# Loading and normalizing the second group of rows between the modulation weights

## The chip, the cores and the metric

The kernel runs on one core of one Trainium2 chip. The metric is device time in microseconds (us) of one launch; lower is better. TensorE is written PE, VectorE DVE, ScalarE ACT, GpSimd POOL and SyncE SP, as in the rows below; SP issues every DMA of this kernel, in one order.

## What is computed

One inference step of a one-layer encoder for two request groups: 1024 prompt rows and 64 sample rows of width 1024, all in 32-bit floats. The part around the change is the first RMS norm, its modulation, and the projection:

```
def modulate(c, w_ada, b_ada):
    m = jax.nn.silu(c) @ w_ada + b_ada
    return jnp.split(m[:, None, :], 6, axis=-1)     # shift1, scale1, gate1, shift2, scale2, gate2
def pre(x, g, shift, scale):
    return rmsnorm(x, g) * (1.0 + scale) + shift
u = pre(x, g_pre_mix, shift1, scale1) @ w_in        # q | k | v of 4 differential, 8 stick-breaking heads
...
x = x + gate1 * rmsnorm(mix @ w_out, g_post_mix)
x = x + gate2 * rmsnorm(square(relu(h2 @ w_up)) @ w_down, g_post_ffn)
```

## The kernel before

Rows go through in nine tiles x0 to x8 of 128 (x8 holds the 64 sample rows), in three groups g of three tiles: x0 to x2, x3 to x5, x6 to x8. Every product is made of three matmuls on a high and a low part of each operand (`split`, lines 62 to 65: a cast on ACT gives the high part, a subtraction on DVE or POOL the low part). The hidden rows are kept transposed, in eight blocks k of 128 columns, as `h1h` and `h1l`.

The start of the kernel is a pipeline over the adaLN weights that make shift1 and scale1, 8 MB in sixteen tiles of 512 KB (`ada_raw`, lines 128 to 136). They come in quarters q = 0 to 3 of four tiles; quarter q gives the shift and scale (`A1`, `B1`) of blocks 2q and 2q+1. For each quarter PE multiplies the weights by silu(c) (`ada_rows`, line 201, tile `pam`), DVE copies the sums to `Rm` (line 322), PE turns them into columns (line 209, tile `pcm`), DVE finishes `A1` and `B1` (lines 326 to 328), and DVE and ACT write the modulated blocks `xt` (lines 344, 346) and split them. Then `first(k)` (line 357) multiplies block k of the first group by the q, k and v weights of head unit 0 into three PSUM banks `p00`, `p01`, `p02`, which fill up over all eight blocks (lines 303 to 305).

`norm_inplace` (line 153) is the RMS norm of a tile of rows: two squares with a running sum on ACT (line 87), three small operations on POOL (lines 89, 80, 81), and two scalings by the result on DVE (line 158). For x0 to x2 it stands before the weights. For x3 to x5 it stood at the head of `ready_1` (line 579), which then transposes the second group (line 335), modulates and splits it, with the low parts on POOL. x6 to x8 are normed after that.

The code is not run in the order in which it is written: the framework schedules the whole program with a timing model of its own when it is built and fixes each engine's order from it. Buffers of one tag are taken from a free pool: the tag `qk` has ten, which the first ten weight tiles, the rows x3 to x7, and the Q and K tiles share; the last six weight tiles lie in the tag `h` as `ae0` and `ae1`. SP issues at most eight transfers ahead: each one waits for the landing of the one eight places earlier. After the projections come the attention units 0 to 7, the output projection, and the feed-forward layer.

Of the kernel before, what the change touches and what calls it, by code (L numbers as in the profile page):

```python
# [27 lines left out]
NTT = 9  # L28
# [6 lines left out]
def build(tc, I, O):  # L35
# [11 lines left out]
    def big(name, tag, shape, dt=F32R):  # L47
        return sb.tile(shape, dt, tag=tag, name=name, bufs=BUFS[tag])

    def small(shape, name, tag, dt=F32, bufs=2):  # L50
        return sb.tile(shape, dt, tag=tag, name=name, bufs=bufs)
# [4 lines left out]
    def bank(name, tag):  # L56
        return pp.tile([P, 512], F32, tag=tag, name=name)
# [9 lines left out]
    def halves(name, n=2):  # L67
        return [big(f"{name}_{i}", "s", [P, 512], F32) for i in range(n)]
# [9 lines left out]
    def rstd(ss, rows, name, add=EPS, inv=1.0 / D):  # L78
        r = small([P, 1], name, "rs", bufs=4)
        nc.gpsimd.tensor_scalar(r[:rows], ss, inv, add, ALU.mult, ALU.add)  # L80
        nc.gpsimd.tensor_tensor(r[:rows], r[:rows], mhalf[:rows], ALU.pow)
        return r

    def sumsq(srcs, rows, name, scratch):
        ss = small([P, 2], name, "ss", bufs=4)
        for i, (a, jk) in enumerate(zip(srcs, scratch)):
            nc.scalar.activation(jk[:rows, : a.shape[-1]], a, AF.Square, accum_out=ss[:rows, i : i + 1])
        if len(srcs) == 2:
            nc.gpsimd.tensor_tensor(ss[:rows, 0:1], ss[:rows, 0:1], ss[:rows, 1:2], ALU.add)
        return ss[:rows, 0:1]  # L90
# [5 lines left out]
    def x_rows(m):  # L96
        return (x_p[m * P : (m + 1) * P, :], P) if m < 8 else (x_s, TS)
# [16 lines left out]
    def load_x(m):  # L114
        src, rows = x_rows(m)
        x = big(f"x{m}", "qk" if m < 8 else "v", [P, 1024], F32)
        load(x[:rows], src)
        return [x[:, :512], x[:, 512:]]
# [9 lines left out]
    def ada_raw(q, part, half):  # L128
        n = 4 * q + 2 * part + half
        if n < 10:  # L130
            raw = big(f"ar{q}{part}{half}", "qk", [P, 4, 256], F32)
        else:
            raw = eh[(n - 10) // 3][:, (n - 10) % 3]
        c0 = D * part + 256 * q
        load(raw, w_ada[:, 4 * half : 4 * half + 4, c0 : c0 + 256])
        ada_raws[c0, half] = raw
# [9 lines left out]
    xn = []  # L146
# [6 lines left out]
    def norm_inplace(xs, m):  # L153
        rows = x_rows(m)[1]
        jk = [small([P, 512], f"jk{m}{i}", "ah") for i in range(2)]
        r = rstd(sumsq([x[:rows] for x in xs], rows, f"ssa{m}", jk), rows, f"rsa{m}")
        for x in xs:
            nc.vector.tensor_scalar(x[:rows], x[:rows], r[:rows], None, ALU.mult)
# [29 lines left out]
    def ada_rows(c0, name, ps=None, between=()):  # L188


        if ps is None:
            ps = bank("pa" + name, "pj")[:, :256]
        for q in range(2):
            raw = ada_raws.get((c0, q))
            if raw is None:
                raw = big(f"ar{name}{q}", "raw", [P, 4, 256], F32)
                load(raw, w_ada[:, 4 * q : 4 * q + 4, c0 : c0 + 256])
            if q == 1 and between:
                between.pop()()
            for i in range(4):  # L200
                mm(ps[32 * i : 32 * i + 32], lhsT=sc[:, 4 * q + i, :], rhs=raw[:, i, :], start=(q == 0), stop=(q == 1), skip_group_check=True)
            yield 0.5
        return ps
# [81 lines left out]
    def drain(gen):  # L285
        for _ in gen:
            pass
# [10 lines left out]
    def dense_T(ps, w, act, g, ks=range(KT)):  # L298

        n = GRP[g][1]  # L300
        (wh, wl), (hh, hl) = w, act[g]
        for k in ks:
            mm(ps[:, :n], lhsT=wh[:, k, :], rhs=hh[:, k, :n], start=(k == 0), stop=False)  # L303
            mm(ps[:, :n], lhsT=wh[:, k, :], rhs=hl[:, k, :n], start=False, stop=False)  # L304
            mm(ps[:, :n], lhsT=wl[:, k, :], rhs=hh[:, k, :n], start=False, stop=(k == 7))  # L305
            yield 3 * n / 2400
# [12 lines left out]
    def columns(ps, q):  # L319

        R = big(f"Rm{q}", "s", [P, 512], F32)
        nc.vector.tensor_copy(R, ps)
        v = sum_to_columns(R, 4, f"pcm{q}")
        col = lambda c: colE[:, c + 2 * q : c + 2 * q + 2].unsqueeze(2).broadcast_to([P, 2, 2])
        a, b = A1[:, 2 * q : 2 * q + 2, :], B1[:, 2 * q : 2 * q + 2, :]
        nc.vector.tensor_tensor(a, v[:, 2:4], col(16), ALU.add)
        nc.vector.tensor_tensor(b, v[:, 0:2], col(8), ALU.add)
        nc.vector.scalar_tensor_tensor(a, a, 1.0, col(0), ALU.add, ALU.mult)

    def block_T(g, k, tag):  # L330

        ps = bank(f"px{g}{k}", tag)
        for m in range(3 * g, 3 * g + 3):
            rows, off = x_rows(m)[1], (m % 3) * P
            nc.tensor.transpose(ps[:, off : off + rows], xn[m][k // 4][:rows, (k % 4) * P : (k % 4 + 1) * P], ident[:rows, :rows])
        return ps

    def block_mod(ps, g, k, el=None, on_act=False):
        n = GRP[g][1]
        xt = small([P, 512], f"xt{g}{k}", "al")  # L340
        for j, c in ((0, slice(0, min(n, TP - GRP[g][0]))), (1, slice(256, 320)))[: 1 + (g == 2)]:
            a, b = A1[:, k, j : j + 1], B1[:, k, j : j + 1]
            if on_act and j == 0:
                nc.scalar.activation(xt[:, c], ps[:, c], AF.Identity, bias=b, scale=a)
            else:
                nc.vector.tensor_scalar(xt[:, c], ps[:, c], a, b, ALU.mult, ALU.add)
        hi, lo = (t[:, k, :n] for t in hT[g])
        split(xt[:, :n], hi, lo, el=el)
        if g == 2:
            nc.vector.tensor_tensor(hT[g][0][:, k, 320:384], xt[:, 256:320], fr(hi[:, 256:320]), ALU.subtract)  # L350
# [6 lines left out]
    def first(k):  # L357

        for i in range(3):
            drain(dense_T(PS[i], PW[0, i], hT, 0, (k,)))  # L360
# [6 lines left out]
    def first_weights(half, up=False):  # L367
        ks = slice(4 * half, 4 * half + 4)
        for i in range(3):
            c = unit_cols(0)[i]  # L370
            if up:
                load(w0[i][:, ks], w_in[:, ks, c : c + P])
                continue
            split(w0[i][:, ks], *(t[:, ks] for t in PW[0, i]), el=nc.vector)

    for q in range(4):
        for part, half in ((0, 0), (0, 1), (1, 0), (1, 1)):
            if q + part:
                ada_raw(q, part, half)
        if q < 2:  # L380
            first_weights(q, True)
    pend = []
    for q in range(4):
        if q < 2:
            first_weights(q)
        for k in (2 * q, 2 * q + 1):
            px[k] = block_T(0, k, ("tr", "qk", "pv")[k % 3])
        ps = bank(f"pam{q}", "pj")
        for part in range(2):
            drain(ada_rows(D * part + 256 * q, f"m{q}{part}", ps[:, 256 * part : 256 * part + 256], pend))  # L390

        def work(ps=ps, q=q):
            columns(ps, q)
            for k in (2 * q, 2 * q + 1):
                block_mod(px[k], 0, k, None, k % 2 == 1)

        pend.append(work)
        if q == 3:
            pend.pop()()
        elif q >= 1:  # L400
            first(2 * q - 2)
            first(2 * q - 1)
    for k in range(4, KT):
        first(k)
    xn += [load_x(m) for m in range(3, NTT)]


    lam4 = small([P, 4, 64], "lam4", "ah")
# [168 lines left out]
                PW[u + 1, i] = proj_weights(u + 1, i)  # L577

    def ready_1():
        for m in range(3, 6):  # L580
            norm_inplace(xn[m], m)
        for k in range(KT):
            block_mod(block_T(1, k, "tr"), 1, k, nc.gpsimd, k % 2 == 1)

# [421 lines left out]
    cost = [st.cost for st in steps]  # L1006
    drain(proj(0, 0))
    ready_1()
    for m in range(6, 9):
        norm_inplace(xn[m], m)  # L1010
# [64 lines left out]
    for m in range(NTT):  # L1075
# [25 lines left out]
        xn = halves(f"xn{m}")  # L1101
# [196 lines left out]
```

## Time and profile before

| | |
|---|---|
| median of 3 runs | 1563.65 us (1562.17 to 1564.41) |
| the profiled execution's own time | 1566.6 us |
| its span | 1564.9 us |
| PE busy | 1504.1 us, 96% of the span |
| DVE, ACT, POOL busy | 59%, 45%, 22% |
| DMA moved | 133.20 MB, mean 85 GB/s |

The span runs from the first to the last instruction; 1.7 us of the execution's own time lie around it. In the first 40th of the span PE is 60% busy, and from the third on 90% or more almost throughout. DMA is 90% busy in the first 40th, 30% or less in most others.

### The profile page before, as it was taken

To read this page: it belongs to the slowest core of one execution; us is meant where nothing else is said; L and a number is where in the kernel's file an instruction comes from. 1 tells how busy PE (TensorE), PEld (TensorE's weight loads), DVE (VectorE), ACT (ScalarE), POOL (GpSimd) and SP (SyncE) were. 2 spreads that over 40 slices of the span, in tenths; PEclk is the share of its full clock that TensorE was granted. 3 is DMA by queue.
4 is the path that set the end of the run, shared out by engine and by line. 5 is a ranking of instruction groups with operands and counts; after the bars stand their busy time and mean duration, and the time that the engine had idled before them with its cause. 6 is when DMAs were issued, how large, how long until landed. Compare 5 with 4: busy or idle time off the path is not lost.

```text
span 1564.9 us, 23485 instructions
## 1 busy us (share of the span) xinstructions
PE 1504.1 (96%) x8714; PEld 1344.9 (86%) x8714; DVE 919.8 (59%) x1761; ACT 702.6 (45%) x1650; POOL 339.0 (22%) x519
## 2 busy tenths in 40 slices
PE   6899999999999999799999999999999999999998
PEld 3689898989989888678899988899899899899896
DVE  3776768676768577775553454444554544544447
ACT  3866766667666576656654112212122111221132
POOL 1553443535152323442110000000000000000002
PEclk9999999999999999799999999999999999999999
DMA  9322343433232215343221222111111111111025
GB/s 314 117 61 83 93 120 91 131 94 108 67 97 74 82 59 167 106 139 132 76 60 41 68 81 81 56 53 41 54 54 41 29 42 52 55 53 43 28 81 181
DMA packets 152516, 133.20 MB, mean 85 GB/s; under 512 B 11233, under 2 KB 136274, under 8 KB 152402
## 3 DMA queue, kind: packets, MB, share of 16 engines
q1 hardware_dynamic: 152402, 131.71, 27.4%
q8 instruction: 68, 1.11, 0.3%
q14 instruction: 46, 0.38, 0.1%
HBM read 108.59 MB, written 23.09 MB: 84 GB/s over the span
## 4 chain that ended last, share of the span: by engine, by line
PE 77%; DVE 6%; issue 5%; ACT 4%; POOL 2%; DMA 2%; POOLq 0%; DVEq 0%; ACTq 0%; SPq 0%
PE pu L303 8%; PE pu L305 8%; PE pu L304 8%; PE pd L1173 8%; PE pd L1174 8%; PE pd L1176 7%; PE pt L604 2%; PE pq L303 2%; PE pq L305 2%; PE pq L304 2%; PE pk L304 2%; PE pk L303 2%; PE pk L305 2%; PE pv L303 2%; PE pv L304 2%
## 5 line engine op out<-in xcount | busy, mean ns | idle before, releaser
L1180 DVE TENSOR_TENSOR acc<-pd,acc 128x512 f32<-128x512 f32 x252 | 171.8, 687 | 113.7 <-PE pd L1176 107.9
L1158 ACT ACTIVATE sq<-pu 128x384 f32<-128x384 f32 (+1 forms) x96 | 45.1, 470 | 309.3 <-PE pu L305 309.3
L1159 DVE TENSOR_TENSOR sq<-sq 128x384 f32<-128x384 f32 (+1 forms) x96 | 72.1, 751 | 172.9 <-ACT sq L1158 172.9
L65 DVE TENSOR_TENSOR al<-pt,ah 128x512 fp32r<-128x512 f32 (+2 forms) x128 | 75.3, 599 | 30.7 <-ACT ah L64 28.7
L593 PE MATMUL pz<-K,Q 128*128 128x512 f32 (+2 forms) x192 | 72.2, 378 | 7.4 <-DVE mn L678 2.4
L64 ACT CAST ah<-pt 128x512 fp32r<-128x512 f32 (+2 forms) x128 | 65.4, 521 | 29.5 <-PE pt L604 24.1
L604 PE MATMUL pt<-ident,s 128*128 128x128 f32 x432 | 69.6, 277 | 0.8 <-issue 0.4
L594 PE MATMUL pz<-Kl,qz 128*128 128x512 f32 (+2 forms) x192 | 65.9, 349 | 0.0
L642 ACT ACTIVATE s<-s,mn 128x512 f32<-128x512 f32 (+3 forms) x96 | 58.5, 612 | 15.5 <-DVE mn L678 14.5
L743 DVE TENSOR_TENSOR_SCAN s<-k,s 128x128 f32<-128x128 f32 (+1 forms) x64 | 53.0, 836 | 13.6 <-ACT k L767 7.7
L65 DVE TENSOR_TENSOR rl<-sq,rh 128x384 fp32r<-128x384 f32 x64 | 35.7, 558 | 38.1 <-ACT rh L64 38.1
L766 ACT ACTIVATE s<-pz 128x512 f32<-128x512 f32 (+2 forms) x96 | 47.6, 496 | 20.9 <-PE pz L594 15.5
L604 PEld LDWEIGHTS pt<-ident,s 128*128 128x128 f32 x432 | 50.0, 142 | 3.8 <-issue 0.6
L442 POOL CAST qz<-Q 64x256 fp32r<-64x256 f32 x64 | 31.2, 488 | 92.9 <-PE pz L594 84.0
L593 PEld LDWEIGHTS pz<-K,Q 128*128 128x128 f32 x192 | 36.4, 190 | 17.2 <-DVE mn L678 6.1
L64 ACT CAST rh<-sq 128x384 fp32r<-128x384 f32 x64 | 32.8, 513 | 40.2 <-DVE sq L1159 38.2
L767 ACT ACTIVATE k<-pz 128x512 f32<-128x512 f32 (+2 forms) x96 | 47.7, 497 | 2.0 <-DVE s L743 0.9
L789 PE MATMUL po<-al,V 128*128 128x256 f32 (+1 forms) x160 | 42.3, 299 | 5.3 <-DVE al L65 5.0
L770 POOL TENSOR_SCALAR_AFFINE_SELECT s<-s 128x128 f32<-128x128 f32 x64 | 30.2, 475 | 75.8 <-ACT s L766 75.2
L788 PE MATMUL po<-ah,V 128*128 128x256 f32 (+1 forms) x160 | 44.8, 294 | 0.4 <-DVE ok L467 0.3
L743 DVE TENSOR_TENSOR_SCAN s<-k,s,s 128x512 f32<-128x512 f32 x32 | 43.4, 1355 | 0.4
L64 ACT CAST r<-sq 128x320 fp32r<-128x320 f32 x32 | 14.8, 461 | 62.6 <-DVE sq L1159 62.6
(1232 smaller groups left out, 5145.5 us busy)
## 6 DMA issues: line engine op xcount, KB each, us to landing
arr<-in_w_ada SPq DMA_DIRECT2D x16, 512.0 KB
arm<-in_w_ada SPq DMA_DIRECT2D x16, 512.0 KB
ar<-in_w_ada SPq DMA_DIRECT2D x10, 512.0 KB
mixD<-mx SPq DMA_DIRECT2D x32, 128.0 KB
xr<-in_x_prompt SPq DMA_DIRECT2D x16, 256.0 KB
xD<-xr SPq DMA_DIRECT2D x16, 256.0 KB
xy<-xD SPq DMA_DIRECT2D x8, 512.0 KB
out_y_prompt<-xy SPq DMA_DIRECT2D x16, 256.0 KB
```

The lines of the kernel that those rows point to most:

```text
L64: (eh or nc.scalar.copy)(hi, src)
L65: (el or nc.vector).tensor_tensor(lo, src, fr(hi), ALU.subtract)
L303: mm(ps[:, :n], lhsT=wh[:, k, :], rhs=hh[:, k, :n], start=(k == 0), stop=False)
L304: mm(ps[:, :n], lhsT=wh[:, k, :], rhs=hl[:, k, :n], start=False, stop=False)
L305: mm(ps[:, :n], lhsT=wl[:, k, :], rhs=hh[:, k, :n], start=False, stop=(k == 7))
L593: mm(ps[:, :w], lhsT=S["Q"][m][:, qt], rhs=S["Kd"][m][:, c0 : c0 + w], start=True, stop=False)
L604: nc.tensor.transpose(pt[:kr, i * P : (i + 1) * P], a, ident)
L743: nc.vector.tensor_tensor_scan(d, k, d, 0.0 if c == n - 1 else s[c + 1][:, 0:1], ALU.mult, ALU.add)
L1173: mm(ps, lhsT=rh[:, off : off + P], rhs=wh[:, cols], start=(j == 0), stop=False)
L1174: mm(ps, lhsT=rh[:, off : off + P], rhs=wl[:, cols], start=False, stop=(m == 8 and end))
L1176: mm(ps, lhsT=rl[:, off : off + P], rhs=wh[:, cols], start=False, stop=end)
L1180: nc.vector.tensor_tensor(acc[m][:, cols], ps, acc[m][:, cols], ALU.add)
```

## The change

The loads of x3, x4 and x5 move ahead of the third quarter's weights, and their norm moves from `ready_1` to after the point where the weights of the third quarter (q = 2) are multiplied. Nothing is computed in another way.

```diff
@@ the loop over quarters @@
     for q in range(4):
+        if q == 2:
+            xn += [load_x(m) for m in range(3, 6)]
         for part, half in ((0, 0), (0, 1), (1, 0), (1, 1)):
             if q + part:
                 ada_raw(q, part, half)
...
         elif q >= 1:
             first(2 * q - 2)
             first(2 * q - 1)
+        if q == 2:
+            for m in range(3, 6):
+                norm_inplace(xn[m], m)
     for k in range(4, KT):
         first(k)
-    xn += [load_x(m) for m in range(3, NTT)]
+    xn += [load_x(m) for m in range(6, NTT)]
...
     def ready_1():
-        for m in range(3, 6):
-            norm_inplace(xn[m], m)
         for k in range(KT):
             block_mod(block_T(1, k, "tr"), 1, k, nc.gpsimd, k % 2 == 1)
```

What this does to the schedule shows in three queues. On SP, from the last weights of unit 0 on, before (`ar200`, `ar201`, `ae0`, `ae1` are the eight weight tiles of quarters 2 and 3, `lam4` small constants):

```order
L135 DMA ar200_191<-in_w_ada 128x4x256
L135 DMA ar201_193<-in_w_ada 128x4x256
L135 DMA ae0_78<-in_w_ada 128x4x256 x3
L135 DMA ae1_79<-in_w_ada 128x4x256 x3
L117 DMA x3_457<-in_x_prompt 128x1024
L117 DMA x4_459<-in_x_prompt 128x1024
L117 DMA x5_461<-in_x_prompt 128x1024
L117 DMA x6_463<-in_x_prompt 128x1024
L117 DMA x7_465<-in_x_prompt 128x1024
L117 DMA x8_467<-in_x_sample 64x1024
L410 DMA lam4_469<-in_lambda_q1 128x64
```

and in the changed kernel (`T0` is a table of attention unit 0, `wq1r` and `wk1r` weights of unit 1):

```order
L117 DMA x3_191<-in_x_prompt 128x1024
L117 DMA x4_193<-in_x_prompt 128x1024
L117 DMA x5_195<-in_x_prompt 128x1024
L135 DMA ar200_197<-in_w_ada 128x4x256
L135 DMA ar201_199<-in_w_ada 128x4x256
L135 DMA ae0_78<-in_w_ada 128x4x256 x3
L135 DMA ae1_79<-in_w_ada 128x4x256 x3
L117 DMA x6_496<-in_x_prompt 128x1024
L117 DMA x7_498<-in_x_prompt 128x1024
L117 DMA x8_500<-in_x_sample 64x1024
L884 DMA Tst0_1752<-in_dist_s 128x64
L670 DMA T0_670<-in_dist 128x1024
```

The eight weight tiles stand three places later, x6 to x8 where they stood, and `lam4` behind `T0`, `wq1r` and `wk1r`.

On ACT, in quarters 2 and 3, before (`jk` are the squares of a row tile, `xt` and `h1h` modulation and split, `Q00` and `kf00` the first evictions of the products):

```order
L344 ACTIVATE xt05_387<-px05_303,B1_122,A1_121 128x384
L64 CAST h1h0_115<-xt05_387 128x384
L64 CAST h1h0_115<-xt04_383 128x384
L87 ACTIVATE jk30_538,ssa3_540<-x3_457 128x512
L87 ACTIVATE jk31_539,ssa3_540<-x3_457 128x512
L87 ACTIVATE jk40_549,ssa4_551<-x4_459 128x512
L344 ACTIVATE xt07_417<-px07_364,B1_122,A1_121 128x384
L87 ACTIVATE jk41_550,ssa4_551<-x4_459 128x512
L64 CAST h1h0_115<-xt06_413 128x384
L64 CAST h1h0_115<-xt07_417 128x384
```

and in the changed kernel:

```order
L87 ACTIVATE jk60_635,ssa6_637<-x6_496 128x512
L87 ACTIVATE jk61_636,ssa6_637<-x6_496 128x512
L87 ACTIVATE jk70_646,ssa7_648<-x7_498 128x512
L344 ACTIVATE xt05_426<-px05_309,B1_122,A1_121 128x384
L87 ACTIVATE jk71_647,ssa7_648<-x7_498 128x512
L64 CAST h1h0_115<-xt04_422 128x384
L64 CAST h1h0_115<-xt05_426 128x384
L87 ACTIVATE jk80_657,ssa8_659<-x8_500 64x512
L87 ACTIVATE jk81_658,ssa8_659<-x8_500 64x512
L344 ACTIVATE xt07_456<-px07_403,B1_122,A1_121 128x384
L64 CAST h1h0_115<-xt07_456 128x384
L64 CAST h1h0_115<-xt06_452 128x384
```

The squares of x6 and the first of x7 stand ahead of quarter 2's modulation, those of x8 ahead of quarter 3's; those of x3 to x5 stand earlier still. Before, the last four squares stood behind `Q00`, between the evictions.

On DVE, at the modulation of quarter 1 and at that of quarter 3, the changed kernel has:

```order
L158 TENSOR_SCALAR x3_191<-x3_191,rsa3_372 128x512 x2
L158 TENSOR_SCALAR x4_193<-x4_193,rsa4_383 128x512 x2
L158 TENSOR_SCALAR x5_195<-x5_195,rsa5_394 128x512 x2
L326 TENSOR_TENSOR A1_121<-pcm1_320,colE_112 128x4
L327 TENSOR_TENSOR B1_122<-pcm1_320,colE_112 128x4
L328 SCALAR_TENSOR_TENSOR A1_121<-A1_121,colE_112 128x4
L346 TENSOR_SCALAR xt02_328<-px02_244,A1_121,B1_122 128x384
```

```order
L346 TENSOR_SCALAR xt06_452<-px06_399,A1_121,B1_122 128x384
L158 TENSOR_SCALAR x8_500<-x8_500,rsa8_663 64x512 x2
L419 TENSOR_TENSOR lam4_502<-lam4_502 128x64
L65 TENSOR_TENSOR h1l0_116<-xt07_456,h1h0_115 128x384
L419 TENSOR_TENSOR lam4_502<-lam4_502 128x64
L65 TENSOR_TENSOR h1l0_116<-xt06_452,h1h0_115 128x384
L346 TENSOR_SCALAR xt10_575<-px10_571,A1_121,B1_122 128x384
```

Before, no scaling stood ahead of quarter 1's `A1`, and the first multiply of `lam4` came after both `h1l0` of quarter 3. Further down the order of all engines is changed in small pieces up to attention unit 6, and is the same from there on; the set of instructions is the same.

## Rows read from the trace of the kernel before

**Rows 1.** The page: busy time of PE, and the chain's shares by engine.

```profile
PE 1504.1 (96%) x8714; PEld 1344.9 (86%) x8714; DVE 919.8 (59%) x1761; ACT 702.6 (45%) x1650; POOL 339.0 (22%) x519
...
PE 77%; DVE 6%; issue 5%; ACT 4%; POOL 2%; DMA 2%; POOLq 0%; DVEq 0%; ACTq 0%; SPq 0%
```

**Rows 2.** Busy time by stretch: from:to and its length, five engines, clock, DMA, GB/s.

```profile
14.00:20.00 6.00, 2.54 (x24) 1.01 (x22) 2.58 (x6) 1.85 (x3) 0.00 (x0) 1.00 1.09 359
20.00:25.00 5.00, 4.25 (x34) 2.16 (x35) 2.71 (x8) 1.59 (x3) 0.00 (x0) 0.70 1.11 347
25.00:30.00 5.00, 5.00 (x26) 3.76 (x25) 2.49 (x4) 1.85 (x3) 0.00 (x0) 0.62 1.08 364
...
40.00:50.00 10.00, 9.71 (x76) 8.36 (x76) 6.43 (x18) 8.28 (x21) 3.02 (x9) 1.00 0.89 282
...
55.00:60.00 5.00, 3.74 (x14) 2.84 (x13) 3.40 (x8) 4.93 (x12) 1.99 (x5) 0.66 0.13 39
60.00:70.00 10.00, 9.36 (x56) 8.48 (x57) 8.16 (x22) 7.02 (x19) 7.40 (x8) 1.00 0.01 2
...
510.00:560.00 50.00, 44.00 (x279) 40.34 (x279) 30.58 (x50) 29.26 (x71) 19.18 (x28) 0.91 0.31 93
```

**Rows 3.** Timeline of SP's DMA issues: start, duration, what.

```profile
39.57 0.33 SPq L410 DMA_DIRECT2D lam<-in_lambda_k  x1
40.85 0.33 SPq L410 DMA_DIRECT2D lam<-in_lambda_q  x1
...
43.41 0.33 SPq L881 DMA_DIRECT2D Tst<-in_dist_s  x1
```

**Rows 4.** What SP's issues waited for: us in total, times, longest.

```profile
SPq L410 <- DMA ae<-in_w_ada: 2.0, 2, 1.1
SPq L410 <- DMA x<-in_x_prompt: 1.9, 2, 0.9
```

**Rows 5.** Timeline of PE: quarter 2's first weights, and the first group's products.

```profile
30.78 0.64 PE L201 MATMUL pam<-ar,sc 128*32 128x256 f32 x8
31.35 1.05 PE L209 MATMUL pcm<-sel,Rm 128*128 128x2 f32 x8
...
35.02 0.44 PE L303 MATMUL p<-h1h,w00h 128*128 128x384 f32 x1
...
39.67 1.05 PE L209 MATMUL pcm<-sel,Rm 128*128 128x2 f32 x8
...
42.92 0.44 PE L303 MATMUL p<-h1h,w00h 128*128 128x384 f32 x1 [0.29 <-ACT h1h L64]
...
50.37 0.34 PE L305 MATMUL p<-h1h,w20l 128*128 128x384 f32 x1
```

**Rows 6.** Timeline: norm of x3 from square to scaling; last two scalings.

```profile
42.77 0.62 ACT L87 ACTIVATE jk<-x 128x512 f32<-128x512 f32 x1
...
44.32 0.19 POOL L89 TENSOR_TENSOR ssa<-ssa 128x1 f32<-128x1 f32 x1 [30.60 <-ACT jk L87]
...
45.78 0.87 DVE L158 TENSOR_SCALAR x<-x,rsa 128x512 f32<-128x512 f32 x2
...
54.86 1.63 DVE L158 TENSOR_SCALAR x<-x,rsa 128x512 f32<-128x512 f32 x2
...
60.10 2.26 DVE L158 TENSOR_SCALAR x<-x,rsa 64x512 f32<-64x512 f32 x2
```

**Rows 7.** Groups on ACT, 42 to 60 us: busy us, mean ns, idle before.

```profile
L87 ACT ACTIVATE jk<-x 128x512 f32<-128x512 f32 (+1 forms) x12 | 7.5, 627 | 0.3
...
L87 ACT ACTIVATION_READ_ACCUMULATOR jk<-x 128x1 f32 (+1 forms) x12 | 2.3, 188 | 0.0
```

**Rows 8.** Timeline of ACT: the first eviction, and the second group's last cast.

```profile
50.19 0.47 ACT L488 ACTIVATE Q<-p 64x384 fp32r<-64x384 f32 x1
...
68.53 0.53 ACT L64 CAST h1h<-xt 128x384 fp32r<-128x384 f32 x1
```

## The prediction

> **What bounds the kernel now.** I read the page first: PE is busy 96% of the span and holds 77% of the chain that ended last [rows 1]. Only a change in PE's idle time, or in the clock that it is granted, can move the end. So the next view is busy time by stretch [rows 2]. The start is the loosest part: PE is busy 2.54 of 6 us at 14 to 20 us, while DMA moves 359 GB/s, and 3.74 of 5 us at 55 to 60 us. Between them, from 40 to 50 us, it is nearly full (9.71 of 10), and from 60 to 70 us again (9.36).
>
> Who holds PE in the loose parts? At first the adaLN weights. SP's small loads are a clock for landings, as each waits for the transfer eight places ahead: the issues of `lam4` ended waits on the last weight tiles and on x3 and x4 [rows 4]. They read: last weight tile down at 39.57, x3 at 40.85, x5 at 43.41 [rows 3]. So a row tile takes 1.28 us (40.85 - 39.57), and the longest of the two waits on weights, 1.1 us behind an issue of 0.33, gives about 1.43 for a weight tile of the same size. PE is then late by itself: it starts the last quarter's columns well after the landing and runs products from 42.92 to 50.71 (50.37 + 0.34) almost without a gap [rows 5]. From 50 us the binding engine is ACT: 4.93 us of 5 at 55 to 60 us [rows 2], with the norm's squares among the evictions that PE waits for.
>
> **The change, part by part.** It adds and removes no instruction; all is in the order.
>
> *Loads.* The eight weight tiles of quarters 2 and 3 slide behind three row tiles, 3 x 1.28 = 3.85 us. The last one lands at 43.4 (x5's old place), x6 and x7 land one and two row tiles later, 44.7 and 46.0. The first of the eight comes down four places ahead of the old last weight, with three of the tiles before it being rows: 39.57 - 4 x 1.43 - 3 x 0.15 = 33.4. PE was ready for it at 30.78 [rows 5], so PE stands still for 2.6 us. Behind it in PE's queue stands `pcm` of quarter 1, which has nothing to do with that weight; it slides along, to end at 31.35 + 1.05 + 2.6 = 35.0.
>
> *Scalings of x3 to x5 on DVE.* They stand ahead of quarter 1's `A1`. x3 lands at about 29.4. A tile's two squares take 1.5 us (42.77 to the sum at 44.25; POOL starts at 44.32), and the scaling starts 1.5 us after them, at 45.78, for 0.87 us [rows 6]. Three tiles in a row: squares until 33.9, scaling of x5 at 35.4 to 36.3. So `A1` waits from 35.0 to 36.3, 1.3 us more, and behind it ACT's `xt`, both casts, and PE's products of block 2: 35.02 + 2.6 + 1.3 = 38.9.
>
> *Products of blocks 2 and 3.* From 35.02 to the next `pcm` at 39.67 are 4.65 us, of which one batch of weights, 0.64 [rows 5], now comes earlier: 4.0 us, at full clock. But PE idled before them. [...] Now it idles 2.6 us and, after `pcm`, about 2.4 us more. The price lies between nothing and twelve of eighteen products at half speed, some 1.7 us. I take 1.5, as the stretch of 14 to 20 us is the nearest row. `pcm` of quarter 2 then starts at 38.9 + 4.0 + 1.5 = 44.4, ends at 45.4.
>
> [...]
>
> *Squares of x6 to x8 on ACT.* Quarter 2's `xt` stands behind both squares of x6 and one of x7, so behind x7's landing at 46.0: it starts at 47.0 though `A1` is there at about 46. Another square, 0.82 us (0.627 + 0.188) [rows 7], stands ahead of the casts. The product of block 4 starts at 48.9 instead of 42.92: 6.0 us late. Quarter 3's `xt` stands behind the squares of x8, which have landed by then. DVE's multiply of `lam4` now stands ahead of the last two `h1l0`, and its loads behind three tiles of 512 KB; I put the landing at 52 to 53 and DVE's need at 53, so no cost, but up to 3 us if it comes later. The products end at 50.71 + 6.1 = 56.8.
>
> *What is given back.* After the first eviction `Q00` ACT no longer holds the four squares of x7 and x8: 4 x 0.82 = 3.3 us off the stretch from 50.19 to the last cast of the second group, at 68.53 + 0.53 = 69.06 [rows 8]. In 60 to 70 us ACT was also idle for 10 - 7.02 = 3.0 us [rows 2], waiting for DVE and POOL, whose queues are shorter by the norms too. Going through the new order with these durations I find about 1.8 of the 3.0 used. Given back: 5.1 us.
>
> The sum: 6.1 - 5.1 = +1.0 us on 1566.6 of the profiled execution, 1567.6. That execution lies 2.95 us above the median of 1563.65, so the median comes to 1564.7.
>
> *Bounds.* Above: nothing is given back, +6.1. Below: no half clock (-1.5) and all of ACT's idle time used (3.0 instead of 1.8, -1.2), and 55 to 60 us at full clock instead of 0.66, 5 x 0.34 = 1.7: 1.0 - 4.4 = -3.4, or 1560.3.
>
> On the scalings: the last two pairs took 1.63 and 2.26 us instead of 0.87 [rows 6], while POOL ran the second group's low parts. [...] I keep ACT as the path.
>
> *The order further down.* Up to unit 6 all engines' orders differ in small pieces. No row prices that. PE's idle time by 50 us shows what order does: 6.0 us in the worst of these stretches, with clock 0.91 [rows 2], near zero in others. I take 0 for the mean and 3 us to either side, half the worst one.
>
> **The rivals.** *Slower, no giving back.* Once the products end at 56.8, PE itself is the bound: at 60 to 70 us it was busy 9.36 of 10 [rows 2], so work that comes 6 us later ends 6 us later, whatever ACT has shed. That gives 1569.8. Its place is PE between the last `p` product and the last second-group product; it decides against "same" once less than 3.0 of the 6.1 us come back. For it speaks 9.36; against it the 1.3 us idle at 55 to 60 us and the half clock there.
>
> *Faster, the norms were the path.* The delay is taken up by PE's own lateness (weights landed at 39.57, products ran until 50.71), while ACT and DVE are free of norms when the second group starts: the lower bound, 1560.3. For it speaks ACT at 4.93 of 5; against it that PE was full from 40 to 50 us with products that the weights gate.
>
> *Order alone decides.* The start comes out even and the changed order down to unit 6 gains or loses 3 us: 1561 or 1567.
>
> *It doesn't do what it says.* If x3 to x5 waited for buffers, nothing would come earlier. Their buffers come free with the first weights, multiplied at 11 us, so I give this nothing.
>
> **How the numbers follow.** About 0.2%, 3.1 us, is what a measurement of this kernel can tell from no change: 1560.5 to 1566.8. The forecast, within that, has 0.54. Slower has 0.29: 0.16 for the rival that gives nothing back, 0.13 for order. Faster has 0.17: 0.08 for the norms, 0.09 for order. The range from 1560.0 to 1569.8 reaches from just under the lower bound to the slower rival; past it lies some 0.1 at either end, where order adds to a rival.
>
> **What the profile after would show.** The loads: the first weight product of quarter 2 at about 33.4 instead of 30.78. DVE: scalings until about 36 and `A1` right behind. ACT: squares of x6 and x7 ahead of `xt` at 47. The products ending at about 56.8; the second group's last cast at about 70. If that cast is at 75, nothing came back; if at 66, the norms were the path. A difference that arises only after 110 us is order. I am wrong in mechanism if the products end before 54, which would mean that weights did not gate PE.

## The result, and the profile after

The changed kernel takes 1585.78 us (median of 4 runs, 1585.24 to 1586.88), the kernel before 1564.03 beside it: a ratio of 1.0137, interval 1.0123 to 1.0151, or 21 us slower. I had forecast 1564.7 and a range that ended at 1569.8. The profiled execution took 1586.88 us, with a span of 1585.1, 20.2 more than before.

The page of the changed kernel, first PE's busy time and the chain's shares [rows 1]:

```profile
PE 1513.1 (95%) x8714; PEld 1353.3 (85%) x8714; DVE 926.9 (58%) x1761; ACT 702.0 (44%) x1650; POOL 338.3 (21%) x519
...
PE 75%; DVE 7%; issue 6%; ACT 5%; POOL 2%; DMA 1%; POOLq 0%; DVEq 0%; ACTq 0%
```

PE holds the chain as before. It is busy 9.0 us more (1513.1 - 1504.1), with the same 8714 matmuls, so it ran slower (a mean granted clock of 0.978 over the span, 0.985 before); and it is idle 11.2 us more, the rest of the 20.2.

Where this arises shows best in the time at which PE starts its n-th matmul, counted in either trace (not always the same matmul, as the orders differ, but as much work). In us, the time in the kernel before, and how much later it is in others (three of them are experiments, told below):

| n | 400 | 600 | 1000 | 1400 | 1800 | 2200 | 2600 | 3000 | 3400 |
|---|---|---|---|---|---|---|---|---|---|
| before | 84 | 117 | 178 | 236 | 297 | 360 | 419 | 482 | 544 |
| changed kernel | +0.9 | +7.1 | +10.2 | +13.1 | +15.9 | +17.0 | +19.8 | +21.8 | +21.0 |
| changed start, order of before | +3.0 | +3.4 | +3.4 | +3.4 | +3.4 | +5.3 | +5.3 | +5.4 | +6.0 |
| start of before, changed order | -3.4 | +2.5 | +5.7 | +8.5 | +11.5 | +11.0 | +14.1 | +14.7 | +15.6 |
| order of before from unit 3 on | +1.6 | +7.8 | +10.9 | +13.7 | +18.4 | +18.4 | +18.4 | +18.3 | +17.7 |

At 84 us, where the start is over, the changed kernel is 0.9 us late. The lag grows in nearly every stretch from there to 480 us and stays where it is afterwards; PE's order differs from that of before up to 523 us. Each row is one execution, and whole executions of one kernel lay 1.6 us (the changed kernel) to 8.2 us (the changed start with the order of before) apart, so a step of 1 or 2 us says little. The row of the start of before with the changed order begins at -3.4: by this count the changed order is the better one up to 84 us, and from there to 544 us it loses 19.0 us (15.6 + 3.4).

### The profile page after: what moved, and what is told of

Read it like the earlier page. It is cut to its first block, busy times and chain, and to the rows that moved or that the text cites. A ratio compares the mean times of both kernels' runs of the same rounds, so it can differ in the third digit from the quotient of the medians.

```text
span 1585.1 us, 23509 instructions
## 1 busy us (share of the span) xinstructions
PE 1513.1 (95%) x8714; PEld 1353.3 (85%) x8714; DVE 926.9 (58%) x1761; ACT 702.0 (44%) x1650; POOL 338.3 (21%) x519
## 4 chain that ended last, share of the span: by engine, by line
PE 75%; DVE 7%; issue 6%; ACT 5%; POOL 2%; DMA 1%; POOLq 0%; DVEq 0%; ACTq 0%
PE pu L303 8%; PE pu L305 8%; PE pu L304 8%; PE pd L1176 8%; PE pd L1177 8%; PE pd L1179 7%; PE pt L607 2%; PE pq L303 2%; PE pq L304 2%; PE pq L305 2%; PE pk L305 2%; PE pk L303 2%; PE pk L304 2%; DVE s L746 2%; PE pv L303 1%
## 5 line engine op out<-in xcount | busy, mean ns | idle before, releaser
L681 DVE CUSTOM_DVE_ANT_0 s<-pz,T 128x512 f32<-128x512 f32 (+3 forms) x64 | 37.1, 586 | 11.6 <-PE pz L597 11.0
```

## Order or start: the two taken apart

**How an order is held.** The framework lets an edge be put between two instructions of one engine that fixes which is issued first and adds no wait. A table gives the order of one kernel for everything written from the projections of unit 0 on, norms excepted, and each instruction gets an edge to the one ahead of it on its engine. The start stays as the framework lays it out. Holding costs little by itself: the kernel before, held in its own order but for one small group of instructions, takes 1564.91 us (ratio 1.0008), and the changed kernel, held in its own order but for one place, 1586.13; both are told below.

```diff
-        build(tc, I, O)
+        build(tc, I, O); hold_order(tc)
...
+def hold_order(tc):
+    insts = tc.nc.cur_bb.bb.instructions
+    a, b, c, d, e = marks
+    part = insts[a:b] + insts[c:d] + insts[e:]
+    dep = mybir.DependencyInfo(mybir.DependencyClass.NoSync, mybir.DependencyReason.DATA)
+    for t in HELD.values():
...
+        for x, y in zip(at, at[1:]):
+            tc.add_manual_dep(part[y], part[x].name, dep, reason="order")
```

**The changed start with the order of before.** (`HELD` is before's order.)

> The changed kernel, loads and norms as in the change, but every instruction written from the projections of unit 0 on (other than the norms) is held, engine by engine, in the order of the kernel before. Theory 'order': the start leaves the second group's last cast 2.8 us later (71.85 instead of 69.06), and the other 17 to 18 us come from the changed order of units 0 to 6; so this kernel takes about 1567 us (1564 to 1570). Rival 'start': the late start itself, with its buffers and transfers shifted, makes everything behind it stall, whatever the order; so this stays near 1585 us. In between, say 1575, both have a share.

Measured: 1571.48 us, ratio 1.0038 (1.0023 to 1.0052), 5.9 us by the ratio.

**The start of before with the changed order.** (The kernel before; `HELD` is the changed kernel's order.)

> The other way round: the start of the kernel before, with everything from the projections of unit 0 on held in the order of the changed kernel. Theory 'order': the order brings its loss along, 1564 + 17 to 18 = about 1582 us (1578 to 1586). Rival 'start': near 1564 us.

Measured: 1578.19 us, ratio 1.0099 (1.0075 to 1.0123), 15.5 us. The two parts, 0.38% and 0.99%, make the 1.37% of both together: start and order add, and the order is nearly three quarters of the loss. Theory "order" held, with its share some 2 us smaller and the start's some 3 us larger than it said (1571.48 lies just above its range, 1578.19 at the lower end of its range).

Busy time by stretch, 85 to 510 us, where the orders differ throughout (engines PE, PEld, DVE, ACT, POOL, then granted clock, DMA share, GB/s). The kernel before, then the changed start with the order of before:

```profile
85.00:510.00 425.00, 415.61 (x2793) 380.65 (x2792) 306.60 (x771) 292.71 (x800) 172.03 (x273) 1.00 0.32 94
```

```profile
85.00:510.00 425.00, 415.58 (x2770) 380.36 (x2769) 303.39 (x764) 291.89 (x798) 169.27 (x271) 0.99 0.31 92
```

The same for the changed kernel, then for the start of before with the changed order:

```profile
85.00:510.00 425.00, 403.94 (x2641) 368.98 (x2641) 296.14 (x738) 274.21 (x759) 163.18 (x261) 0.97 0.30 90
```

```profile
85.00:510.00 425.00, 404.00 (x2658) 369.84 (x2659) 298.84 (x736) 279.45 (x770) 160.91 (x259) 0.98 0.30 90
```

The first number after the length is PE's busy time, the one in brackets its matmuls. With the old order PE is busy 415.6 us in both kernels, with the new one 404.0 in both, whatever the start. In the changed kernel 152 matmuls fewer (2793 - 2641) are done in these 425 us, at 0.149 us each (415.61 / 2793) work for 22.6 us. Of these 11.7 are idle time (425 - 403.94, less 425 - 415.61); the other 10.9 were lost with PE busy, at a clock of 0.97 instead of 1.00. So about half of the loss is waits and half is slow matmuls.

What PE waited for in that stretch, the longest rows (us in total, times, longest), in the changed kernel:

```profile
PE pz L596 <- DVE mn L681: 5.0, 8, 2.4
PE pt L607 <- DVE s L746: 2.5, 1, 2.5
PE ptS L607 <- DVE ss L734: 2.3, 1, 2.3
```

and with the start of before:

```profile
PE pz L593 <- DVE mn L678: 5.3, 7, 2.8
PE pt L604 <- DVE s L743: 2.5, 1, 2.5
PE ptS L604 <- DVE ss L731: 2.5, 1, 2.5
```

The same waits, line by line (numbers of lines shift by 3). In the kernel before, the first of these stands at 1.1 us, and the other two are not among its longest:

```profile
PE pz L593 <- DVE mn L678: 1.1, 4, 0.4
```

**The old order from unit 3 on.** Here only the instructions written from the loop step of unit 3 on are held, by the same means.

> The changed kernel, in which only the instructions written from the loop step of unit 3 on are held in the old order; what lies ahead is free, as in the change. Where unit 3 begins (about 253 us before) the changed kernel is 12.8 us late, at 480 us 22. If the loss is a sum of losses in each stretch, each with its own place in the order, this gives about 1564 + 13 = 1577 us (1574 to 1580). If a lag, once there, feeds further lag in any order, it comes to 1583 or more; if the old order makes up for lag, below 1572.

Measured: 1579.92 us, ratio 1.0106 (1.0079 to 1.0133). The last row of the lag table is this run: the lag grows like the changed kernel's until the instructions of unit 3 take over, 18.4 us at n = 1800, and from there not at all. PE does not get later by being late; each stretch of the order has its own losses. (The profiled execution lies 2.5 us above the changed kernel at n = 1800; this kernel's four executions lie up to 4.9 us apart.)

## Is it this order, or any new one?

Three more orders, laid out freely by the framework. In the first only the loads are moved:

```diff
@@ the changed kernel, loop over quarters @@
-        if q == 2:
-            for m in range(3, 6):
-                norm_inplace(xn[m], m)
@@ ready_1 @@
     def ready_1():
+        for m in range(3, 6):
+            norm_inplace(xn[m], m)
```

> Of the change only the early loads of x3 to x5; their norm stays at the head of ready_1, and the order is free, so it is a third order for units 0 to 6. By 'order' the time can fall anywhere that an order can put it: the start costs some 3 us (the weights land 3.4 us later), and the order adds 0 to 20, so 1567 to 1587, with no reason to equal the changed kernel's. By 'start' it follows the weights: 1567.

Measured: 1577.71 us, ratio 1.0094 (1.0074 to 1.0114). The framework set the squares of x3 to x5 ahead of quarter 1's modulation all the same, because the rows are there: the second half of the change, writing the norm earlier, moves next to nothing at the start. It does make another order further down.

In the second and third, the eviction of K takes its two halves the other way round, first in the kernel before, then in the changed one:

```diff
@@ proj_k @@
-        for m in range(2):
+        for m in (1, 0):
             r, o = slice(64 * m, 64 * m + 64), slice(64 - 64 * m, 128 - 64 * m)
             nc.scalar.copy(Kd[m][r, cols], ps[r, :w])
```

> The kernel before, with its start untouched, and one edit that means nothing for the work: of the two halves of K the one with index 1 is evicted first. The framework lays out another order for units 0 to 6 (the first PE instruction that differs is behind the start). Theory 'any new order costs': the order of before is far better than a usual one, and this loses 10 to 18 us as the other two new orders did, 1574 to 1582. Rival 'the new order of the change was bad luck': orders lie around that of before, 1564 with some 5 us to either side.

Measured: 1572.31 us, ratio 1.0052 (1.0030 to 1.0073): 8 us for an edit without meaning for the result and with the start untouched (PE's order is that of before up to 54 us). What the swap costs in an order that is otherwise that of before was not run.

> The changed kernel with the meaningless edit of the other order experiment: of the two halves of K the one with index 1 is evicted first, the order is free. If the 14 to 18 us of the changed order are one draw of many, another order gives another loss: start 6 plus 4 to 18, so 1574 to 1588, most likely not within 3 us of 1585.8. If the change's late start makes any freely laid out order bad, it stays at 1583 to 1589.

Measured: 1578.38 us, ratio 1.0096 (1.0078 to 1.0115), 6 us faster than the changed kernel by the ratios. If the start costs 5.9 in these too, which was not measured, the four free orders lost about 15 (the change), 9 (the loads alone), 8 and 9 us against the order of before. None was as good. How many would be is not known from four. Shown is that a small edit, even one without meaning, can give the order of before away, and that this costs more than any start tried here.

## One place in the new order

The largest step of the lag, 6.2 us between n = 400 and n = 600, is one place. Timeline of the changed kernel at 100 us, PE, DVE and POOL (start, duration, what, idle before and releaser):

```profile
101.86 0.63 PE L597 MATMUL pz<-Kl,qz 128*128 128x512 f32 x1
104.87 0.76 PE L596 MATMUL pz<-K,Q 128*128 128x512 f32 x1 [2.38 <-DVE mn L681]
...
107.18 0.47 PE L305 MATMUL pv<-h1h,w20l 128*128 128x320 f32 x1
```

```profile
101.40 1.68 DVE L647 TENSOR_TENSOR l<-l 128x1 f32<-128x1 f32 x1
...
104.02 0.69 DVE L681 CUSTOM_DVE_ANT_0 s<-pz,T 128x512 f32<-128x512 f32 x1
```

```profile
100.70 2.36 POOL L65 TENSOR_TENSOR wk1l<-wk1r,wk1h 128x1024 fp32r<-128x1024 f32 x1
```

and the busy times of 102 to 110 us, with PE's granted clock, in the same columns as above:

```profile
102.00:110.00 8.00, 5.62 (x21) 4.77 (x20) 6.41 (x16) 4.00 (x12) 2.86 (x5) 0.50 0.36 121
```

DVE's order has the sum `l` ahead of the next score's reduction. `l`, one column, took 1.68 us and ended with POOL's split of a weight (100.70 + 2.36 = 103.06); behind it stood its reciprocal, `cf`, an eviction of Q, and then at 104.02 the reduction for which PE's next score waited, 2.38 us. PE's granted clock was 0.50 from 102 to 110 us, and 16 of the 24 `pv` products took 0.47 or more instead of 0.31. It did not fall behind this wait: it stood at 0.50 from 100.8 us on, after PE had been idle for 0.16, 0.24 and 0.52 us between the scores ahead.

```profile
100.80:102.50 1.70, 1.69 (x3) 0.68 (x3) 1.56 (x3) 1.65 (x7) 1.70 (x1) 0.50 0.56 164
```

With the start of before and the changed order both rows are there again, on DVE and on PE:

```profile
97.09 1.68 DVE L644 TENSOR_TENSOR l<-l 128x1 f32<-128x1 f32 x1 [0.17 <-ACT s L642]
```

```profile
100.56 0.77 PE L593 MATMUL pz<-K,Q 128*128 128x512 f32 x1 [2.85 <-DVE mn L678]
```

In the kernel before, DVE has the reduction ahead of `l`, and PE has the transposes `pnk` and four pairs of `po` between the scores (DVE's rows, then PE's):

```profile
101.80 0.69 DVE L678 CUSTOM_DVE_ANT_0 s<-pz,T 128x512 f32<-128x512 f32 x1
...
102.42 0.15 DVE L644 TENSOR_TENSOR l<-l 128x1 f32<-128x1 f32 x1
```

```profile
99.50 0.44 PE L459 MATMUL pnk<-ident,kf 128*128 128x128 f32 x2
...
102.65 0.47 PE L593 MATMUL pz<-K,Q 128*128 128x512 f32 x1 [0.74 <-DVE l L644]
103.08 0.41 PE L303 MATMUL pv<-h1h,w20h 128*128 128x320 f32 x1
```

So I changed this one place: the changed kernel's own order held, but with two moves in the tables. On PE the 24 `pv` products go ahead of the waiting score `pz`; on DVE the eviction of Q and the reduction go ahead of the sum `l`.

> The changed kernel, its own order held from the projections of unit 0 on, but for one place at 100 us. There DVE had the sum l, its reciprocal and cf ahead of an eviction of Q and a score's reduction, PE waited 2.38 us for that reduction, its clock fell from 101 to 111 us, and the 24 matmuls of pv, which stood behind the wait, ran at half speed. Here DVE does Q and the reduction first, and PE has the 24 pv matmuls ahead of the waiting score. Theory 'stalls and their clock': the lag that arises between 84 and 117 us falls from 6.2 us to about 0, and the end comes 5 to 6 us earlier, about 1580 us. Rival 'the time is only moved': another wait takes its place within some 20 us, and the end stays within 1.5 us of 1585.8.

Measured: 1586.13 us, ratio 1.0133 (1.0113 to 1.0153). The rival held. The trace of this kernel shows the wait that took its place, on PE and then on DVE:

```profile
104.40 0.63 PE L303 MATMUL pv<-h1h,w20h 128*128 128x320 f32 x1 [3.04 <-DVE Kl L519]
```

```profile
102.02 0.15 DVE L647 TENSOR_TENSOR l<-l 128x1 f32<-128x1 f32 x1
...
103.92 0.43 DVE L519 TENSOR_TENSOR Kl<-pk,K 64x256 fp32r<-64x256 f32 x1
```

`l` now takes 0.15 us and the reduction is done at 102.02, but `pv` waits 3.04 us for a PSUM bank that the second eviction of K (`Kl`, 103.92) holds, and runs at a clock of 0.50 (102 to 109 us) as before, 0.47 us for a product. PE has nothing else there: the `po` pairs that filled this stretch in the kernel before stand ahead of it in the new order, `pnk` behind it. So one instruction in front of another was not the cause. That the cause is which work is left for PE when ACT and DVE are behind fits these rows, but it is argued: no run put the `po` pairs or `pnk` back there.

## The start by itself

With the order of before held, the start costs 5.9 us, not the +1.0 of my sum. Two edits to it. In the first the squares of x6 to x8 are kept behind quarter 3's casts on ACT:

```diff
-    for m in range(6, 9):
-        norm_inplace(xn[m], m)
+    with tc.issue_after(last): [norm_inplace(xn[m], m) for m in range(6, 9)]
```

> The changed kernel with the order of before held from unit 0 on, and the squares of x6 to x8 kept behind the last casts of quarter 3 on ACT. So quarter 2's xt no longer waits for x7. Theory: block 4's product comes at about 46.2 instead of 49.8, the first group's products end near 55 instead of 60.6, and of the 6 to 7 us that the start cost with this order (1571.5) some 3 to 5 go: 1566 to 1568. Rival: the squares then stand among the evictions and take the gain back, 1571.

Measured: 1570.17 us, ratio 1.0030 (1.0016 to 1.0045), not told apart from 1.0038. Its timeline, PE then ACT:

```profile
46.55 0.45 PE L303 MATMUL p<-h1h,w00h 128*128 128x384 f32 x1 [0.28 <-ACT h1h L64]
...
59.60 0.90 PE L464 MATMUL pnk<-ident,kf 128*128 128x128 f32 x3 [5.30 <-ACT kf L514]
```

```profile
53.21 0.26 ACT L420 ACTIVATE lam<-lam 128x64 f32<-128x64 f32 x1 [1.55 <-DVE lam L419]
...
58.11 0.47 ACT L493 ACTIVATE Q<-p 64x384 fp32r<-64x384 f32 x1
```

The product of block 4 comes at 46.55, as expected, and the first group's products end at 54.3; then PE waits 5.30 us for the eviction `kf`, since ACT has the squares and `lam4`, whose load came late, in front of it. What is taken from one end of ACT's queue comes back at the other. The second edit loads x3 to x5 one quarter later (`if q == 3` for `if q == 2`), and keeps the first:

> As the kernel with the late norms of x6 to x8 and the order of before, but x3 to x5 are loaded one quarter later, ahead of the fourth quarter's weights. Quarter 2's weights then land as before; only quarter 3's come 3.8 us later, of which PE's products of blocks 4 and 5 cover all but some 2. Six squares leave the stretch between 42 and 60 us, where ACT is the bound. Theory: products end at about 52.7, the second group at about 68 to 69, and the time is 1563 (1560 to 1566). Rival: PE is held 2 us and nothing comes back, 1567.

Measured: 1568.29 us, ratio 1.0022 (1.0008 to 1.0035): above the forecast of 1563, at its rival's end. Then `lam4` in addition was loaded ahead of all this, in both kernels, and in the kernel before, whose order was held whole for it:

```diff
+    lam4 = small([P, 4, 64], "lam4", "kf")
     for q in range(4):
+        if q == 2:
+            for i, n in enumerate(("lambda_q1", "lambda_k1", "lambda_q2", "lambda_k2")):
+                load(lam4[:, i, :], I[n][0].partition_broadcast(P))
```

> The kernel with early x3 to x5, late squares of x6 to x8 and the old order (1570.2), with lam4 loaded ahead of x3 in addition. There lam4's load waited 6 us on SP for a buffer that ACT's queue held, ACT waited 2.5 us for it among the evictions, and PE waited 5.3 us for the eviction kf. Theory 'lam4 blocks ACT': PE's wait falls to 1 or 2 us and the time to about 1566 to 1567. Rival: ACT's squares alone hold the evictions, 1570.

Measured: 1570.70 us, ratio 1.0040 (1.0025 to 1.0056).

> The same addition to the kernel that loads x3 to x5 ahead of the fourth quarter's weights (1568.3): by 'lam4 blocks ACT' 1564 to 1565.5, by the rival 1568.

Measured: 1568.61 us, ratio 1.0023 (1.0008 to 1.0037).

> The kernel before with the order of every engine held as it is, except that lam4 is loaded ahead of the third quarter's weights (into a buffer of its own tag kf) and its products, sums and exponential are done there. In before, ACT spent 2.4 us on them (two of 0.45, a table load of 1.28, 0.20) among the evictions at 50 to 60 us. Theory 'ACT's queue at the evictions sets the start': about 2 us come off, 1561.5 to 1563. Rival 'ACT's time there is not on the path': 1564 as before.

Measured: 1564.91 us, ratio 1.0008 (0.9995 to 1.0020): no change that can be told. In the first of the three, PE's wait for `kf` fell from 5.30 to 0.46 us as expected, but the weights came later:

```profile
34.43 0.64 PE L201 MATMUL pam<-ar,sc 128*32 128x256 f32 x8 [4.05 <-DMA ar<-in_w_ada]
...
59.31 0.55 PE L465 MATMUL pnk<-ident,kf 128*128 128x128 f32 x3 [0.46 <-ACT kf L515]
```

Without the early `lam4` (late squares) SP issued the load of x8 at 37.45 us, and it does at 39.57 here. In the changed kernel, whose SP order is that of late squares up to there, the first weight product of quarter 2 stood at 32.84 after a wait of 1.48 us, and it stands at 34.43 here, after 4.05. The four small loads, issued from 21.41 us on ahead of x3, take four of the eight places of SP's queue. So these runs don't say what `lam4` alone costs. No start tried beats that of before: 1564 to 1565 stays the best time. What makes up the 5.9 us beyond the 3 to 3.7 that three of the traces with the old order (the changed start, late squares, late loads) show at 84 us stays open; in the trace of the first, two more came in one stretch, with a granted clock of 0.52 from 342 to 345 us.

## Why the prediction was wrong

Timeline of the changed kernel's start: PE, DVE, ACT.

```profile
32.84 0.64 PE L201 MATMUL pam<-ar,sc 128*32 128x256 f32 x8 [1.48 <-DMA ar<-in_w_ada]
...
39.09 0.57 PE L303 MATMUL p<-h1h,w00h 128*128 128x384 f32 x1
...
43.11 1.05 PE L209 MATMUL pcm<-sel,Rm 128*128 128x2 f32 x8
...
49.77 0.69 PE L303 MATMUL p<-h1h,w00h 128*128 128x384 f32 x1 [3.69 <-ACT h1h L64]
...
52.92 0.52 PE L305 MATMUL p<-h1h,w00l 128*128 128x384 f32 x1
...
60.25 0.34 PE L305 MATMUL p<-h1h,w20l 128*128 128x384 f32 x1
```

```profile
33.95 0.88 DVE L158 TENSOR_SCALAR x<-x,rsa 128x512 f32<-128x512 f32 x2 [0.71 <-POOL rsa L81]
34.75 0.15 DVE L326 TENSOR_TENSOR A<-pcm,colE 128x4 f32<-128x4 f32 x1
...
48.16 0.88 DVE L158 TENSOR_SCALAR x<-x,rsa 128x512 f32<-128x512 f32 x2 [2.88 <-ACT jk L87]
```

```profile
47.42 0.63 ACT L87 ACTIVATE jk<-x 128x512 f32<-128x512 f32 x1 [0.48 <-DMA x<-in_x_prompt]
...
48.05 0.65 ACT L344 ACTIVATE xt<-px,B,A 128x384 f32<-128x384 f32 x1
...
71.34 0.51 ACT L64 CAST h1h<-xt 128x384 fp32r<-128x384 f32 x1
```

**Loads: right.** The first weight of quarter 2 is multiplied at 32.84; I said 33.4 [rows 5 for before].

**Scalings: right in place, too dear.** They stand ahead of quarter 1's `A1`, but it starts at 34.75, when `pcm` (33.41 to 34.46) is just done. x3 was squared from 27.69 on, not from 29.4. The 1.3 us were 0.3.

**Products of blocks 2 and 3: 38.9 was met by luck.** They start at 39.09, but not because of the scalings: the casts were done at 36.83. PE first had six transposes and a batch of weights in its queue, and there the half clock was:

```profile
36.60:39.10 2.50, 2.50 (x19) 1.35 (x15) 0.87 (x2) 0.22 (x1) 0.00 (x0) 0.50 1.10 347
```

The products behind them took 0.34 us each but for the first, so the 1.5 us of slow clock that I put on them was not on them, and `pcm` of quarter 2 starts at 43.11 instead of 44.4. The 1.5 us were my estimate, and no run shows that figure: in the changed kernel the first nine of the eighteen took 1.80 us (39.09 to 40.89), and with late squares and the early `lam4`, where PE had waited 4.05 us for the weights, 3.00 (42.64 to 45.64), 1.2 more.

**Squares of x6 to x8 on ACT: right.** `xt` waits for the square of x7 at 47.42, and starts at 48.05 (I said 47.0, since I had x7 down at 46.0); block 4's product comes at 49.77, 6.85 us late; I said 6.0.

**The half clock: too small, and left out where the wait is longest.** PE was idle 3.69 us ahead of that product, and in 50 to 56 us its granted clock was 0.50 (busy times of the changed kernel by stretch):

```profile
50.00:56.00 6.00, 6.00 (x22) 6.00 (x23) 4.75 (x14) 3.85 (x13) 1.63 (x4) 0.50 0.18 45
```

The products took 0.52 us instead of 0.34, and the first group's end came at 60.59, 9.9 us late instead of 6.1. I had put 1.5 us of slow clock behind the idle times at 30 to 38 us, and none behind the wait that my own sum made ahead of block 4.

**Given back: right in size.** The second group's last cast ends at 71.85 (71.34 + 0.51) instead of 69.06: +2.8 where I said +1.0, so 7.1 of the 9.9 came back, not 5.1. Some of that is the new order's. With the order of before held, the last product and the last cast (PE, then ACT) are

```profile
58.95 0.34 PE L305 MATMUL p<-h1h,w20l 128*128 128x384 f32 x1
```

```profile
71.84 0.53 ACT L64 CAST h1h<-xt 128x384 fp32r<-128x384 f32 x1
```

so the products end 8.6 us late (59.29), the cast 3.3 (72.37), and 5.3 came back. The rival "slower, no giving back" is out in the changed kernel's trace: the lag was 0.9 at 84 us. So is "faster, the norms were the path". With the order of before held the lag is 3.0 at 84 us, and the start costs 5.9: nearly the 6.1 of the first of these rivals, though not by its mechanism, and far from +1.0.

**The order further down: this is the step that failed.** I wrote 0 ± 3 us, "half the worst" stretch of PE's idle time, and gave "order alone decides" 3 us either way. It cost 15.5 us on its own (12 to 19 by its interval). Two things were wrong in it. In the trace of before PE was idle for only 9.4 of 425 us at a clock of 1.00; an order that is so nearly full can lose much and gain little, so the guess should not have been even about zero. And I took one stretch's idle time as the measure of what a reorder can do, though the changed order covers nine such stretches, and left out the clock, which took about as much as the waits. The stretch that I took, 510 to 560 us, also lies almost whole behind the place (523 us) from which PE's order is the same in both kernels. My own sign for it, "a difference that arises only after 110 us is order", held in the main: the lag grew from 98 us on.

## What to carry to other kernels

Where a framework lays out the order from a timing model, an edit to one place is a new order for all that follows, and its time says little about the edit: hold the order, or make the same reorder by a meaningless edit, before you judge it. How full the bound engine is tells the sign of the risk: at 98% busy, at full clock, a new order could win 9.4 us of 425 at most, and the four tried lost. In a queue in order, look at what other work stands between two waiting instructions: at 100 us the kernel before had some there and the changed one had none.

## What the runs showed of the hardware

A DVE sum of two single columns took 1.68 us instead of 0.15, and ended with the POOL subtraction that ran beside it (103.08 and 103.06); in the kernel with that place changed it came after POOL's (99.58 + 2.36 = 101.94) and took 0.15. Before, the last two pairs of scalings took 1.63 and 2.26 us [rows 6], with POOL's low parts of the second group running from 55.21 to 56.21 and from 59.92 to 62.08; x6's pair took 0.88 us in the changed kernel, with POOL idle from 48.13 to 49.40. No run shows that this moved the end.

Over 425 us a clock of 0.97 instead of 1.00 took nearly as much (10.9 us) as the waits (11.7). But the clock did not fall behind every wait, and not only behind long ones. After 3.69 us it was 0.50 from 50 to 56 us. With the start of before and the changed order, the wait of 2.85 us began at 97.7, behind a `pz` of 0.39 us; the next `pz` took 0.77, and the `pv` products took 0.47 instead of 0.31 up to 106.1. In the changed kernel the clock was at 0.50 from 100.8 already, behind gaps of at most 0.52 us, and the wait of 2.5 us for `s` (`pt`, at 410 us) passed at 1.00:

```profile
409.00:415.00 6.00, 3.24 (x26) 2.69 (x25) 5.64 (x7) 3.62 (x10) 4.93 (x5) 1.00 0.09 27
```
